# A planner's prices set anew: POOL's operations and waits, row sums on ScalarE, fp32r matmuls and array part changes

## The chip, the cores and the metric

One core of a Trainium2 chip runs the whole program. The metric is device time in microseconds (us), as the median of several executions; one further execution was taken by the hardware profiler, and all rows below are of that one. The engines are PE (TensorE; its weight loads are PEld), DVE (VectorE), ACT (ScalarE), POOL (GpSimd) and SP, which starts transfers. Each engine works through a queue of its own, strictly in order, and waits at an instruction whose inputs are not ready. So the order in which the program lists instructions decides who waits.

## The reference, cut to what matters

256 tokens of width 1024 go through two blocks.

```python
x = first_block(...)    # hybrid_mixer (SSD scan, attention, convolution), then 32 experts, top 2
return second_block(x, ...)   # rwkv7_time_mix, then diff_attention_mix
def rwkv7_time_mix(...):      # 16 heads of 64
    r, k, v, g = einsum(xmix, w_in);  kk = kk / maximum(norm(kk), 1e-12)
    state, y = scan(step, ...)
    y = (y - mean) * rsqrt(var + GN_EPS) * lnx_g + lnx_b     # per head
def diff_attention_mix(...):  # 8 heads of 2 x 64
    attn = softmax(s0) - lam * softmax(s1)
    o = rms_norm(attn @ v, subln_g) * (1 - lam_init)
h = h + rms_norm(y);  h = h + rms_norm(sigmoid(h @ ple_gate) * (p @ ple_w))
```

What matters here is that the second block has many small reciprocal roots: the norm of `kk` and the group norm in each pair of RWKV heads, and a norm in each attention head. No engine computes them in one instruction here; they are Newton steps.

## The kernel before, in words

Three parts follow each other. **The mixer** (`mixer`, L509) and **the second block** (`second`, L1577) are not written in the order in which they run. They are written as many generators ("streams"), each yielding instructions of one strand of work, and a planner picks the order. **The experts** (`moe`, L1189) between them are written in their order by hand.

The planner is the class `Plan` (L141) with the chooser `Mux` (L329). `Plan` keeps a time for every engine (`at`) and, for each tile region, when its last use ends. An instruction is ready (`ready`, L194, through `when`) at the latest end of what it depends on plus a handover from the table `LAT` (L145), which has one number for each pair of producing and consuming engine. It starts at the later of that and the engine's own time (`start`, L198); on TensorE the price of a change of array part (`change`, L261) comes on top. Its length is from `cost` (L213), in ns, and the table is worked out by engine:

```python
        if eng == "scalar":
            return (51 if psum else 93) + n * 0.835 + 93 * s.pointers(op)
        return 150 + n * 2.1                                    # POOL; n elements a partition
```

`Mux.run` (L362) looks at the head of every stream, finds the earliest planned start, and among the instructions of that engine that could start within a hold (60 ns for TensorE, 120 for DVE and ACT, 150 for POOL, `WAIT`, L54) takes the one of the highest rank. So a planned time is never waited for on the chip; it only decides the place in the queue. `come` (L204) leaves the price of a part change out once TensorE has been on the same kind (fp32 or fp32r) for longer than `LONG` (400 ns for fp32). A matmul's form is its rows and columns rounded to 32, 64 or 128 (`form`, L251).

Most operations are recorded at L76, the line where `Op.go` calls the engine, so tiles tell them apart.

In the second block, `Feed` (L1590) loads a raw weight slab, copies it on ACT to fp32r (`whl<-raw`) and subtracts on DVE for the low part (`whl<-raw,whl`). `dense` multiplies the slabs on TensorE into banks `pd`, at a low rank. The strands with high rank are the heads:

- `rwkv_inner` (eight pairs of heads): norms of `kk` into `nn` (matmuls against `tab`, form 128x64), a Newton step on POOL, then a spread of its result over partitions by matmuls `pm<-ident,rsq_y` (form 128x64).
- `rwkv_invert` and `rwkv_chunks`: a triangular inverse in 64x64 and 32x32 matmuls (`pi`), the chunked scan (`pe`), statistics `bn` on DVE, eight small operations and a Newton step on POOL for n below 6 (on DVE for 6 and 7), then `yn` on DVE and transposes `pe<-ident,yn`.
- `diff_head` (eight heads): scores into `pe`, `e` masked on DVE, exponentials with row sums on ACT, `on` squared with a row sum into `ss`, a Newton step (POOL for n below 6, else DVE), then `on` scaled on DVE and transposed on TensorE (`pi<-ident,on`).
- `Finish` (twice): projection, norms and gates; the product by the gain (`work<-e,gain`, 128x512) runs on POOL.

`newton` (L1670) on POOL is one start operation and three rounds of four, each depending on the one before: 13 small operations on tiles of 2 or 4 columns.

`minus` and `add` (L1643, L1655) could choose DVE or POOL by planned time, but return DVE when `s.alone` is true, as it is in both planned parts. They carry their own copy of POOL's price, which stays.

Of the kernel before, what the change touches and what calls it, by code (L numbers as in the profile page):

```python
# [140 lines left out]
class Plan:  # L141
# [1 line left out]


    LAT = {("vector", "vector"): 127, ("gpsimd", "gpsimd"): 100, ("scalar", "vector"): 133, ("vector", "scalar"): 128,  # L145
           ("scalar", "scalar"): 143, ("scalar", "gpsimd"): 159, ("vector", "gpsimd"): 155, ("gpsimd", "scalar"): 75,
           ("gpsimd", "vector"): 75, ("gpsimd", "tensor"): 200, ("scalar", "tensor"): 225, ("vector", "tensor"): 215,
           ("tensor", "scalar"): 197, ("tensor", "vector"): 197, ("tensor", "tensor"): 0}

# [63 lines left out]
    def cost(s, op):  # L213
        eng, name, out, ins = op.lane.name, op.op, op.outs[0], op.ins
        n = 1
        for _, c in (ins[-1] if name in ("tensor_reduce", "bn_stats") else out).ap[1:]:
            n *= c
        if eng == "tensor":
            if name == "transpose":
                return 109  # L220
            if ins[0].dtype == F32R:
                return max(107, n / 2.4) + 11
            k, m = s.form(op)
            if k == m:
                if k == 128:
                    return max(214, n * 4 / 2.4 + 4)
                return 58 if m == 64 else 31
            if k == 64:
                return max(107, n * 4 / 2.4) * (0.75 if n > 128 else 1) + 2
            if m == 64:  # L230
                return 58 if n < 8 else 165 if n <= 64 else 109
            return 13 if s.box(out)[0] else max(107, n * 2 / 2.4) + 14
        psum = any(x.space == PSUM for x in (out, *ins))
        if eng == "vector":
            fast = name in ("tensor_scalar", "tensor_copy", "memset") and not psum
            return 68 + n * (0.52 if fast else 1.04) + 61 * s.pointers(op)
        if eng == "scalar":
            return (51 if psum else 93) + n * 0.835 + 93 * s.pointers(op)
        if eng == "sync":
            return n * 512 / 355.0  # L240
        return 150 + n * 2.1

    @staticmethod
    def pointers(op):
# [16 lines left out]
    def change(s, op):  # L261

        op = getattr(op, "ops", [op])[0]
        if s.part is None or s.part == s.form(op) or (s.part, s.form(op)) == ((64, 128), (128, 128)):
            return 0
        return 138 if s.cold(s.at.get("tensor", 0.0)) else 95

    def clocked(s, start, dur, op):

# [2485 lines left out]
```

## Time and profile before

| what | us |
|---|---|
| median of 3 executions | 1253.44 |
| lowest, highest | 1244.65, 1255.34 |
| the profiled execution | 1252.17 |
| its span, first to last instruction | 1250.4 |
| busy in the span: PE / DVE / ACT / POOL | 1136.9 / 656.9 / 434.5 / 124.3 |

The span is the profiled execution without what lies around the program, 1.8 us. "Busy" is time in which an engine has an instruction in work; an engine's wait is put down to what ended it. The granted clock is TensorE's, as a share of 2.4 GHz: it has two levels, 1.00 and 0.50.

### The profile page before, as it was taken

The numbers are of one execution on the slowest core, as the hardware profiler recorded it, in microseconds if no ns is written. First come the engines' busy times: TensorE is split into PE (matmuls) and PEld (weight loads), VectorE is DVE, ScalarE is ACT, GpSimd is POOL, SyncE is SP. The second block draws the span as 40 slices with busy tenths as digits, with TensorE's granted clock in tenths as the row PEclk, the third lists the DMA queues.
The fourth block names the chain that finished last, engine by engine and source line by source line (L and its number), as shares of the span: only waits on it lengthen the run. The fifth ranks groups of instructions, "written<-read, shape, count | busy, mean of one in ns | idle before, by whom it ended". The sixth has DMA issues, their size and how long they took to land. (4 is left out here: it accounts for less than half of the span.)

```text
span 1250.4 us, 20460 instructions
## 1 busy us (share of the span) xinstructions
PE 1136.9 (91%) x7902; PEld 783.9 (63%) x7902; DVE 656.9 (53%) x1790; ACT 434.5 (35%) x1081; POOL 124.3 (10%) x358
## 2 busy tenths in 40 slices
PE   5999996999999999898987889999999978998896
PEld 3787786443443434443434788888887655888775
DVE  4586676121111111111113986677777658788785
ACT  3474452111111101110104564343436437455453
POOL 1000000000000000000000031222212011122202
PEclk9899998899999999999997798999999989999998
DMA  8668657799999999999994341122214422443332
GB/s 369 264 235 320 244 210 323 305 420 420 421 420 420 420 420 421 421 420 420 421 419 162 129 162 61 39 76 70 73 52 155 175 76 85 169 148 123 121 109 74
DMA packets 52628, 306.14 MB, mean 245 GB/s; under 512 B 5680, under 2 KB 10288, under 8 KB 25392
## 3 DMA queue, kind: packets, MB, share of 16 engines
q1 hardware_dynamic: 52368, 304.67, 61.7%
q8 instruction: 64, 1.05, 0.3%
q14 instruction: 36, 0.29, 0.1%
q0 software_dynamic: 160, 0.13, 0.1%
HBM read 302.55 MB, written 2.10 MB: 244 GB/s over the span
## 5 line engine op out<-in xcount | busy, mean ns | idle before, releaser
L411 PE MATMUL pgu<-w,xe 128*64 128x512 f32 x1024 | 232.3, 595 | 14.6 <-DMA w<-moe 14.6
L411 PEld LDWEIGHTS pgu<-w,xe 128*64 128x64 f32 x1024 | 80.0, 137 | 154.9 <-issue 116.8
L76 DVE TENSOR_TENSOR whl<-raw,whl 128x512 fp32r<-128x512 f32 x192 | 127.4, 688 | 7.7 <-ACT whl L76 6.5
L76 PE MATMUL pd<-xm,whl 128*128 128x256 f32 x768 | 122.5, 307 | 8.0 <-ACT xm L76 6.5
L76 ACT CAST whl<-raw 128x512 fp32r<-128x512 f32 x192 | 110.6, 619 | 49.0 <-PE pd L76 33.4
L411 PE MATMUL py<-w,condp 128*64 128x512 f32 x480 | 108.4, 596 | 7.0 <-ACT condp L1461 7.0
L76 PEld LDWEIGHTS pd<-xm,whl 128*128 128x128 f32 x768 | 105.7, 205 | 13.6 <-ACT xm L76 7.1
L1486 DVE SCALAR_TENSOR_TENSOR yl<-py,ws,yh 128x512 fp32r<-128x512 f32 (+1 forms) x33 | 24.2, 735 | 121.9 <-ACT yh L1485 121.9
L411 PEld LDWEIGHTS py<-w,condp 128*64 128x64 f32 x480 | 35.8, 137 | 69.2 <-issue 55.0
L1395 POOL TENSOR_TENSOR order<-P,wt 128x256 f32<-128x256 f32 x16 | 9.8, 615 | 615.3 <-PE pw L1466 419.5
L1485 ACT ACTIVATE yh<-py,ws 128x512 fp32r<-128x512 f32 (+1 forms) x33 | 22.1, 674 | 119.1 <-PE acc L411 65.5
L1451 DVE TENSOR_TENSOR condp<-condp,pgu 128x512 f32<-128x512 f32 x15 | 10.3, 687 | 97.6 <-PE pgu L411 97.6
L1450 DVE SCALAR_TENSOR_TENSOR condp<-condp,pgu 128x512 f32<-128x512 f32 x15 | 10.3, 688 | 95.3 <-ACT condp L1449 95.3
L76 PE MATMUL pd<-xx,whl 128*128 128x256 f32 x384 | 58.2, 290 | 1.9 <-ACT whl L76 1.1
L76 PE MATMUL pd<-hh,whl 128*128 128x256 f32 x384 | 58.4, 298 | 1.6 <-ACT whl L76 0.8
L76 PEld LDWEIGHTS pd<-hh,whl 128*128 128x128 f32 x384 | 51.3, 199 | 4.8 <-issue 2.4
L76 PE MATMUL pd<-whl,hh 128*128 128x512 f32 x192 | 52.1, 410 | 2.3 <-ACT hh L76 2.3
L76 PEld LDWEIGHTS pd<-xx,whl 128*128 128x128 f32 x384 | 50.3, 193 | 3.9 <-ACT whl L76 1.3
L76 PE MATMUL a<-hh,wh 128*128 128x256 f32 x160 | 47.7, 298 | 4.9 <-ACT wh L76 4.3
L76 DVE TENSOR_TENSOR wl<-w,wh 128x512 fp32r<-128x512 f32 (+1 forms) x60 | 39.1, 689 | 18.5 <-ACT wh L76 18.4
L76 PE MATMUL a<-hh,wl 128*128 128x256 f32 x160 | 47.4, 296 | 0.0
L76 PE MATMUL a<-hl,wh 128*128 128x256 f32 x160 | 46.8, 293 | 0.0
(511 smaller groups left out, 2187.0 us busy)
## 6 DMA issues: line engine op xcount, KB each, us to landing
w<-moe SPq DMA_DIRECT2D x190, 1024.0 KB, 19.8
w<-ada SPq DMA_DIRECT2D x12, 2048.0 KB, 11.6
raw<-awin SPq DMA_DIRECT2D x32, 512.0 KB, 3.3
raw<-bwin SPq DMA_DIRECT2D x32, 512.0 KB, 3.2
w<-win SPq DMA_DIRECT2D x5, 2048.0 KB, 9.3
raw<-pleg SPq DMA_DIRECT2D x16, 512.0 KB, 3.3
w<-wout SPq DMA_DIRECT2D x2, 2048.0 KB, 7.9
raw<-awout SPq DMA_DIRECT2D x8, 512.0 KB, 3.2
```

Of the source, the lines that this page charges most:

```text
L76: r = s.fn(*s.a, **s.k)
L411: return s.nc.tensor.matmul(out, lhsT=lhsT, rhs=rhs, start=first, stop=last, **kw)
L1395: G.tensor_tensor(PW.rearrange(four, e=2), P[:, :, o:o + 128].bitcast(F32).rearrange(four, e=2), wt[:, :, 2 * i:2 * i + 2, None].to_broadc ...
L1450: V.scalar_tensor_tensor(hid, hid, 1.0, pgu[0], op0=OP.add, op1=OP.mult)
L1451: V.tensor_tensor(hid, hid, pgu[1], op=OP.mult)
L1485: A.activation(y[0], p, AF.Copy, scale=ws)
L1486: V.scalar_tensor_tensor(y[1], p, ws, y[0].bitcast(F32), op0=OP.mult, op1=OP.subtract)
```

## The change

Five prices change: what POOL reads from ACT or DVE counts as ready 500 ns after its end; a POOL operation counts 170 ns plus its elements; an ACT operation with a second output (a row sum, `accum_out`) counts 92 ns more; an fp32r matmul counts its columns at 2.35 in place of 2.4 a ns; and at the upper clock a change of array part costs 115 ns out of 64x64, 60 out of 128x64 and 95 out of the others, in place of 95 for all.

```diff
     LAT = {("vector", "vector"): 127, ("gpsimd", "gpsimd"): 100, ("scalar", "vector"): 133, ("vector", "scalar"): 128,
-           ("scalar", "scalar"): 143, ("scalar", "gpsimd"): 159, ("vector", "gpsimd"): 155, ("gpsimd", "scalar"): 75,
+           ("scalar", "scalar"): 143, ("scalar", "gpsimd"): 500, ("vector", "gpsimd"): 500, ("gpsimd", "scalar"): 75,
...
             if ins[0].dtype == F32R:
-                return max(107, n / 2.4) + 11
+                return max(107, n / 2.35) + 11
...
         if eng == "scalar":
-            return (51 if psum else 93) + n * 0.835 + 93 * s.pointers(op)
+            return (51 if psum else 93) + n * 0.835 + 93 * s.pointers(op) + 92 * (len(op.outs) > 1)
         if eng == "sync":
             return n * 512 / 355.0
-        return 150 + n * 2.1
+        return 170 + n * 2.1
...
         if s.part is None or s.part == s.form(op) or (s.part, s.form(op)) == ((64, 128), (128, 128)):
             return 0
-        return 138 if s.cold(s.at.get("tensor", 0.0)) else 95
+        if s.cold(s.at.get("tensor", 0.0)):
+            return 138
+        return {(64, 64): 115, (128, 64): 60}.get(s.part, 95)
```

## Rows read from the trace of the kernel before

**Rows 1.** Busy time by stage: stretch, its length, busy us by engine, PEclk, DMA share, GB/s.
```profile
core 0: us, PE busy (x) PEld busy (x) DVE busy (x) ACT busy (x) POOL busy (x), PEclk, DMA share, GB/s
0.00:225.00 225.00, 194.79 (x1378) 159.62 (x1379) 146.71 (x472) 102.68 (x253) 6.41 (x17) 0.93 0.71 283
...
690.00:960.00 270.00, 257.36 (x2772) 220.91 (x2773) 209.40 (x585) 123.00 (x317) 63.20 (x233) 0.93 0.25 84
960.00:1085.00 125.00, 111.62 (x648) 83.46 (x648) 87.06 (x252) 63.23 (x156) 8.29 (x5) 0.95 0.38 133
1085.00:1200.00 115.00, 101.79 (x747) 90.54 (x745) 94.26 (x232) 59.96 (x182) 28.18 (x79) 0.97 0.37 127
1200.00:1250.40 50.40, 40.35 (x186) 31.89 (x185) 33.59 (x88) 20.72 (x47) 8.34 (x5) 0.94 0.27 94
```

**Rows 2.** Waits, PE from 1085 to 1200, DVE from 690: total, times, longest.
```profile
PE pi L76 <- DVE on L76: 11.0, 7, 2.1
...
DVE on L76 <- POOL rsq_y L76: 10.1, 6, 2.0
```

**Rows 3.** Waits of PE from 690 to 960.
```profile
PE pm L76 <- POOL rsq_y L76: 2.7, 1, 2.7
PE pe L76 <- DVE yn L76: 1.8, 3, 0.8
```

**Rows 4.** Timeline of one attention head: start, us, engine, operation, idle before.
```profile
1087.39 0.16 DVE L76 TENSOR_SCALAR ss<-ss 128x2 f32<-128x2 f32 x1
...
1090.61 0.68 DVE L76 TENSOR_TENSOR whl<-raw,whl 128x512 fp32r<-128x512 f32 x1
...
1087.63 0.55 POOL L76 TENSOR_SCALAR rsq_i<-ss 128x2 int32<-128x2 int32 x1 [42.25 <-DVE ss L76]
...
1090.62 0.72 POOL L76 TENSOR_TENSOR rsq_t<-rsq_t,ss 128x2 f32<-128x2 f32 x1
1091.43 0.19 POOL L76 TENSOR_SCALAR rsq_t<-rsq_t 128x2 f32<-128x2 f32 x1
...
1092.80 0.19 POOL L76 TENSOR_TENSOR rsq_y<-rsq_y,rsq_t 128x2 f32<-128x2 f32 x1
...
1093.60 0.41 PE L76 MATMUL pi<-ident,on 128*128 128x128 f32 x2 [2.06 <-DVE on L76]
1093.77 2.75 PE L76 MATMUL pd<-hh,whl 128*128 128x256 f32 x12
```

**Rows 5.** Timeline of POOL, first and last of an RWKV chunk's 21 operations.
```profile
852.88 0.20 POOL L76 TENSOR_TENSOR mu<-bn 128x4 f32<-128x4 f32 x1 [6.82 <-DVE bn L76]
...
858.74 0.20 POOL L76 TENSOR_TENSOR rsq_y<-rsq_y,rsq_t 128x4 f32<-128x4 f32 x1
```

**Rows 6.** Busy time and PEclk behind the wait, and PE's timeline later in that stage.
```profile
1093.95:1097.35 3.40, 3.40 (x17) 2.78 (x15) 2.02 (x4) 1.77 (x6) 0.00 (x0) 0.50 0.28 83
...
1162.32 2.13 PE L76 MATMUL pd<-hh,whl 128*128 128x256 f32 x9
...
1129.12 3.14 PE L76 MATMUL pd<-hh,whl 128*128 128x256 f32 x24
```

**Rows 7.** The chain that ended last: start, us, what.
```profile
743.50 4.47 PE pd L76 x27
...
1233.70 6.91 PE pd L76 x30
```

**Rows 8.** Groups of POOL and ACT: count, busy us, mean ns, idle before.
```profile
L76 POOL TENSOR_TENSOR work<-e,gain 128x512 f32<-128x512 f32 x8 | 10.7, 1340 | 31.1 <-DVE e L76 31.1
...
L76 ACT ACTIVATION_READ_ACCUMULATOR e<-e,mx 128x1 f32 x32 | 6.0, 187 | 0.0
```

**Rows 9.** Timeline of PE: one spread of eight whole, another in three pieces.
```profile
749.61 0.66 PE L76 MATMUL pm<-ident,rsq_y 128*64 128x128 f32 x8
...
845.89 0.43 PE L76 MATMUL pm<-ident,rsq_y 128*64 128x128 f32 x2
...
847.66 0.43 PE L76 MATMUL pm<-ident,rsq_y 128*64 128x128 f32 x2
...
848.93 0.44 PE L76 MATMUL pm<-ident,rsq_y 128*64 128x128 f32 x4
```

## Prediction

> **What bounds the kernel now.** I read the busy times by stage first [rows 1]. The program has three parts: the mixer (to 225 us), the experts (225 to 690) and the second block (690 to the end). TensorE (PE) is busy 195 of 225 us in the first and 511 of 560 in the last, so it is the bound there and only its idle time, or a slower clock, can be won. The experts' order is written by hand and reads none of the numbers that change. The mixer uses POOL for 6.4 us in all. In the second block POOL works 63 us in the RWKV stage (690 to 960) and 28 us in the heads of the differential attention (1085 to 1200). What the new numbers can move is there.
>
> Next I read who waits for whom. In the heads PE stands 11.0 us in seven waits for `on`, and DVE stands 10.1 us in six waits for POOL's `rsq_y`, right ahead of `on` [rows 2]. In the RWKV stage PE waits once 2.7 us for `rsq_y`, and three times, 1.8 us in all, for `yn`, which reads a `rsq_y` too [rows 3]. With six sevenths of the 11.0 (one of those heads has its Newton step on DVE) 2.7 + 1.8 + 9.4 = 13.9 us of PE stand behind POOL.
>
> The timeline of one head shows why [rows 4]. DVE ends `ss` at 1087.55 (1087.39 + 0.16), and POOL's thirteen operations of the Newton step end at 1092.99: 5.44 us. The planner of before counts 155 + 13 x 154 + 12 x 100 = 3.36 us (a 128x2 operation is 150 + 2 x 2.1 ns). So it lists `on` 2.1 us too early in DVE's queue and `ident,on` as early in PE's. Both engines work their queues in order, so DVE stands (one of the six waits above), and PE stands 2.06 us with work listed behind that could have run, twelve projections `pd`.
>
> **The change part by part.** No instruction is added or removed, and none changes its engine: the two helpers that choose between DVE and POOL always return DVE, since `s.alone` is true in both planned parts. Only the order on each engine moves.
>
> *POOL's wait and POOL's operations.* What POOL reads from DVE or ACT counts as ready 500 ns after its end instead of 155 or 159, and each POOL operation counts 20 ns more. A head's Newton step is planned 345 + 13 x 20 = 605 ns later, at 3.97 of the 5.44 us that it takes. For an RWKV chunk, eight small operations and a Newton step, the plan was 155 + 9 x 158 + 12 x 258 = 4.67 us and becomes 500 + 9 x 178 + 12 x 278 = 5.44; the trace has 852.88 to 858.94, 6.06 us [rows 5]. So both plans stay short, but less. The 500 ns are not the trace's handover (1087.55 to 1087.63, under 0.1 us), they stand in for slow first operations of 0.55 us; the pace of a step is right: from 1091.43 to 1092.80 five steps take 0.274 us each [rows 4], the new number is 174 + 100.
>
> In the heads, then, six waits get shorter by at most 0.605, 3.6 us. PE has work to put in, since the `pd` behind `ident,on` wait for nothing that is late. What speaks against the whole 3.6 is in the same rows: a POOL operation takes 0.72 us while DVE runs `whl<-raw,whl`, the first one 0.55, and 0.19 once DVE stands still [rows 4]. If DVE fills its gap with one more `whl`, one POOL operation becomes 0.36 to 0.53 us longer; at 0.4, six chains give 2.4 us back. The filler may also read PSUM, or be none, so I take half of that: 3.6 - 1.2 = 2.4 us, ends 0 and 3.6.
> The Trainium skill (SBUF — State Buffer, section "Who interferes with whom") says that a DVE instruction with two inputs in SBUF contends with a POOL instruction that reads SBUF, and that of the two sharing a port pair the second waits out the first. This trace agrees, with 0.72 us beside `whl` and 0.19 alone. By that rule a constant price for POOL cannot be right in both states, and a slot that is filled lengthens what it was to wait out: with every slot so filled the heads would win 1.2 us, without it 3.6.
>
> *The clock behind the longest waits.* After the wait of 2.06 us the granted clock of the next 3.4 us is 0.50, its lower level of 1.2 GHz: twelve `pd` take 2.75 us, and behind the fifth wait nine take 2.13, where 24 take 3.14 at the upper level, 0.13 each [rows 4, 6]. That is 2.75 - 1.57 = 1.2 and 2.13 - 1.18 = 0.95 us. Shorter waits may spare these 2.1 us; half is 1.0, ends 0 and 2.1.
>
> *RWKV.* The wait of 2.7 us shrinks by 0.6. The 27 `pd` in the chain behind it take 4.47 us, 0.166 each [rows 7], for 0.13: 1.0 us of clock, which I count at half, for a wait of 2.1 would be as long as those after which the clock fell. Of the three `yn` waits (1.8 us) I take 1.2; the plan moves by 0.77 each, which covers them unless others come. Together 0.6 + 0.5 + 1.2 = 2.3 us, ends 0 and 4.
>
> *The products by gain on POOL in the two finishing stages.* Eight, planned at 1.23 us plus 0.155, now 1.25 plus 0.5, measured 1.34 [rows 8] after a handover under 0.1: planned 0.3 us too late rather than too early. Their reader waits for a sum of squares and a Newton step of DVE besides, which hides it. Cost zero; with the cover gone, 8 x 0.3 = 2.4 us lost.
>
> *Row sums on ScalarE.* 92 ns more for each activation with a sum. The trace has the reading of the sum as an operation of its own, 187 ns [rows 8], partly beside the activation, so 92 is nearer than nothing. It shifts the heads' exponentials by 0.18 us a pair. Zero, ends -1 and +1 us.
>
> *Fp32r matmuls* (N / 2.35 in place of N / 2.4). 256 columns go from 118 to 120 ns, 512 from 224 to 229; thirty 512-column ones take 6.91 us, 230 each [rows 7]. PE's planned time gets right by 2%; by itself that moves nothing. The mixer is touched by this and the sums alone, and PE stands 30 us there [rows 1], mostly for weights and chains with nothing to fill in. Zero, ends -3 and +3 us, a tenth of that.
>
> *Changes of array part.* 115 ns out of 64x64 and 60 out of 128x64, each 95 before. The price only decides which of several ready matmuls goes first. Zero; what it can cost is rival C.
>
> Sum: 2.4 + 1.0 + 2.3 = 5.7 us. Not all of it gets to the end: the finishing stages (960 to 1085, and from 1200) are chains in which PE stands 13.4 and 10.1 us, and DVE is busy 82% in the heads [rows 1]. I count nine tenths, 5.1 us. The profiled execution has 1252.17 us, 1.8 more than its span of 1250.4, and the median shown is 1.3 above it. So 1247.1 for such an execution, and by the median **1248 us**.
>
> **Rivals.**
> *A. Given back.* The waits for POOL keep their length because DVE's filler blocks POOL, or the next stage waits by as much. For it: slow POOL operations stand beside DVE work [rows 4]. Against: some 0.4 is given back for 0.605. Gain 0 to 1 us: 1253. The skill's rule above is this rival.
> *B. The waits go.* A shift lets all 13.9 us behind POOL go, with 3.1 us of the lower clock: 1253 - 17 = 1236. For it: filler lies right behind each wait. Against: the new plan is still 1.5 us short in each head.
> *C. Slower, by broken batches.* PE's window for preferring a higher stream is 60 ns. A price of 95 kept a 128x64 batch whole against it; 60 does no longer. Place: the RWKV heads' `st` and spread batches and the chunks' pairs, some ten seams in each of eight heads, 80. Price: a spread of eight takes 0.66 us whole; broken into 2, 2 and 4 it takes 0.43 + 0.43 + 0.44 = 1.30 [rows 9], so 0.32 a break. From 16 further breaks on the forecast's gain is gone; 30 give 1248 + 9.6 = 1258, all 80 give 1274. Against: batches are broken already, and the planner drops the price after 400 ns on the same kind of matmul.
> That the change does nothing would need every order to stay; 605 ns are five `pd`, so it won't.
>
> **How the numbers follow.** Forecast (a gain of 1 to 12 us) 0.46, A 0.20, B 0.16, C 0.18. One per cent, 12.5 us, is about what a measurement of this kernel can tell from no change. Faster by that: 0.14 of B and 0.08 of the forecast's and the mixer's far ends, 0.22. Slower by that: half of C, 0.09. Same: 0.69. The range goes from just under B, 1235, to 1261, which holds C up to 40 breaks and the unknown costs of the mixer and of the gain products.
>
> **What would show it.** Right: PE's waits for `on` near 8 us instead of 11.0, DVE's for `rsq_y` near 7 instead of 10.1, more `pd` ahead of `ident,on`, no fall of the clock behind the heads' waits. By A POOL's slow operations become more and the waits stay. By C the 128x64 groups stand in more and shorter pieces from 690 to 960, and that stage is longer. I am wrong if the difference sits in the mixer, or if the RWKV stage moves by over 5 us either way.

## The result, and the profile after

The changed kernel takes 1235.9 us (median of 4, 1233.2 to 1238.8) where the kernel before takes 1251.8 beside it: ratio 0.9883, 95% interval 0.9857 to 0.9909. That is 15 us less, 11 to 18 by the interval, where the prediction had 5. The profiled execution has a span of 1237.1 us, 13.3 less than before.

No instruction was added or removed, so the first thing to compare is what the same instructions cost. The page's busy times of the changed kernel:

```profile
PE 1125.5 (91%) x7902; PEld 774.2 (63%) x7902; DVE 656.2 (53%) x1790; ACT 434.4 (35%) x1081; POOL 121.9 (10%) x358
```

TensorE's 7902 matmuls take 11.4 us less (1136.9 before); its idle time, span less busy, went from 113.5 to 111.6. So of 13.3 us about 11.4 are the same matmuls running quicker and only 1.9 are waits. Added up from the clock records, TensorE spent 112.1 us of the whole span at its lower level before and 88.6 after. The prediction had looked for waits first.

To see where, I cut both traces at the same events: the first operation of the experts, the first projection `pd`, the end of the last `yn`, and, as bounds of the attention heads, the first matmul `xx,whl` and the first matmul `whl,hh` behind the last `on`. Busy times in the three stretches that count (mixer; RWKV; heads): the stretch, its length, PE, PEld, DVE, ACT, POOL, granted clock, DMA. The kernel before:

```profile
0.00:219.95 219.95, 190.58 (x1358) 155.38 (x1358) 145.60 (x470) 101.84 (x251) 5.79 (x16) 0.94 0.71 281
690.53:1002.18 311.65, 297.49 (x3042) 247.47 (x3043) 237.70 (x683) 140.58 (x354) 63.20 (x233) 0.94 0.28 97
1051.31:1206.13 154.82, 136.98 (x991) 122.11 (x992) 124.24 (x312) 84.09 (x246) 28.18 (x79) 0.97 0.39 135
```

The changed kernel:

```profile
0.00:217.97 217.97, 187.95 (x1358) 153.39 (x1358) 145.14 (x470) 101.73 (x251) 5.81 (x16) 0.97 0.72 284
688.82:993.13 304.31, 289.66 (x3043) 240.19 (x3043) 236.93 (x682) 140.78 (x355) 60.40 (x233) 0.96 0.30 99
1040.62:1192.48 151.86, 136.19 (x991) 122.28 (x992) 124.67 (x312) 84.34 (x246) 29.24 (x79) 0.97 0.42 137
```

The mixer is 2.0 us shorter, RWKV 7.3, the heads 3.0; the pieces between and behind give the rest. In the mixer TensorE's idle time (length less PE busy) did not fall either, 29.4 before and 30.0 after. In RWKV it is 14.2 before and 14.7 after: nothing was won on waits there. Its busy time fell by 7.8 us for one and the same 3042 or 3043 matmuls, and the granted clock rose from 0.94 to 0.96. In the heads it is the other way round: the clock is 0.97 in both, and idle went from 17.8 to 15.7.

The waits that answer to [rows 2] and [rows 3], of the changed kernel, waits in total, times, longest:

```profile
PE pi L76 <- DVE on L76: 8.6, 6, 1.8
...
DVE on L76 <- POOL rsq_y L76: 8.2, 6, 1.6
...
PE pm L76 <- POOL rsq_y L76: 2.0, 1, 2.0
```

And the head of [rows 4] after the change:

```profile
1077.18 0.17 DVE L76 TENSOR_SCALAR ss<-ss 128x2 f32<-128x2 f32 x1
...
1077.44 0.56 POOL L76 TENSOR_SCALAR rsq_i<-ss 128x2 int32<-128x2 int32 x1 [43.35 <-DVE ss L76]
...
1082.43 0.19 POOL L76 TENSOR_TENSOR rsq_y<-rsq_y,rsq_t 128x2 f32<-128x2 f32 x1
...
1082.66 0.42 DVE L76 TENSOR_TENSOR on<-pq,rsq_y 128x256 f32<-128x256 f32 x1 [0.82 <-POOL rsq_y L76]
...
1083.23 0.41 PE L76 MATMUL pi<-ident,on 128*128 128x128 f32 x2 [0.83 <-DVE on L76]
```

Here DVE waits 0.82 us and PE 0.83, where PE waited 2.06. POOL's thirteen operations take about as long as they did (5.18 us from the first start to the last end, 5.36 before); other work now stands ahead of `on`.

### The profile page after: what moved, and what is told of

Same layout as the page of the kernel before. It is cut to its first block, busy times and chain, and to the rows that moved or that the text cites. A ratio compares the mean times of both kernels' runs of the same rounds, so it can differ in the third digit from the quotient of the medians.

```text
span 1237.1 us, 20470 instructions
## 1 busy us (share of the span) xinstructions
PE 1125.5 (91%) x7902; PEld 774.2 (63%) x7902; DVE 656.2 (53%) x1790; ACT 434.4 (35%) x1081; POOL 121.9 (10%) x358
## 5 line engine op out<-in xcount | busy, mean ns | idle before, releaser
L413 PE MATMUL pgu<-w,xe 128*64 128x512 f32 x1024 | 232.3, 595 | 14.7 <-DMA w<-moe 14.7
L76 PE MATMUL pd<-xm,whl 128*128 128x256 f32 x768 | 117.7, 301 | 8.1 <-ACT xm L76 6.6
L76 PEld LDWEIGHTS pd<-xm,whl 128*128 128x128 f32 x768 | 102.5, 200 | 13.4 <-ACT xm L76 7.2
L1453 DVE TENSOR_TENSOR condp<-condp,pgu 128x512 f32<-128x512 f32 x15 | 10.3, 688 | 97.7 <-PE pgu L413 97.7
L1452 DVE SCALAR_TENSOR_TENSOR condp<-condp,pgu 128x512 f32<-128x512 f32 x15 | 10.3, 689 | 95.4 <-ACT condp L1451 95.4
## 6 DMA issues: line engine op xcount, KB each, us to landing
w<-wout SPq DMA_DIRECT2D x2, 2048.0 KB, 10.5
```

Source lines behind the costliest of these rows:

```text
L76: r = s.fn(*s.a, **s.k)
L413: return s.nc.tensor.matmul(out, lhsT=lhsT, rhs=rhs, start=first, stop=last, **kw)
L1452: V.scalar_tensor_tensor(hid, hid, 1.0, pgu[0], op0=OP.add, op1=OP.mult)
L1453: V.tensor_tensor(hid, hid, pgu[1], op=OP.mult)
```

## The experiments

I held three theories. P: the waits behind POOL are what was won, so POOL's prices alone do it. J: the prices together make the plan right, and any order planned from them is good. R, later narrowed to S: some of it belongs to single prices, and the rest is what this one order happens to draw.

### Each price alone

```diff
e1: -("scalar", "gpsimd"): 159, ("vector", "gpsimd"): 155    +500, 500;   -return 150 + n * 2.1   +return 170 + n * 2.1
e2: -return 138 if s.cold(...) else 95                       +{(64, 64): 115, (128, 64): 60}.get(s.part, 95) when not cold
e3: -max(107, n / 2.4) + 11                                  +max(107, n / 2.35) + 11
e4: -(51 if psum else 93) + n * 0.835 + ...                  +... + 92 * (len(op.outs) > 1)
```

> The kernel before with POOL's two prices alone changed (500 ns of wait, 170 ns an operation). Theory P (the waits behind POOL are what was won): it takes most of the 14.6 us, ratio near 0.990; DVE's waits for rsq_y in the heads near 8 us as in the changed kernel, and the RWKV stage shorter by 5 to 7 us. Theory R (any new order of this kernel moves the time by several us either way, and the sum of the parts is not the whole): heads about 2.5 us shorter, RWKV stage anywhere within 5 us of before, ratio 0.993 to 1.002.

> The kernel before with the prices of array part changes alone changed (115 out of 64x64, 60 out of 128x64). Theory P: no part of the gain, within 2 us of before. The third rival of the prediction: slower by up to 10 us, with the 128x64 groups in more pieces. Theory R: within 6 us of before either way, all of it in the RWKV stage; the waits behind POOL unchanged.

> The kernel before with the price of fp32r matmuls alone changed (2.35 for 2.4). Theory P: within 2 us of before. Theory M (the mixer's 1.7 us and some of the RWKV stage come from TensorE's planned time, that is now right by 2%): the mixer 1.5 to 2 us shorter and in all 3 to 6 us faster. Theory R: within 6 us either way.

> The kernel before with the price of ScalarE's row sums alone changed (92 ns more). Theory P: within 2 us of before, the heads at most 0.5 us shorter, RWKV unchanged, since only the heads, the finishing stages and the mixer have such sums. Theory R: the same bound of 2 us in the heads, but the mixer may move by 2 us.

Measured against the kernel before: POOL's prices 0.9994 (0.9972 to 1.0015), part changes 0.9995 (0.9971 to 1.0019), fp32r 1.0049 (1.0028 to 1.0071), sums 1.0003 (0.9983 to 1.0023). Three are nothing and one is slower, and together they are 0.9883. P falls, and so does any account in which the parts add up. So does M, the theory held for e3 that the fp32r price wins 3 to 6 us by itself. With POOL's prices alone DVE's waits for `rsq_y` did fall to 8.1 us and the heads to 146.9 us, 8 less; but RWKV came out at 318.3, 7 more, beyond the 5 that R had allowed. With the sums alone the mixer came out at 226.5, 7 more where R had allowed 2. With the part price alone the heads came out at 148.7, 6 less, though R had put all of a change into RWKV; the waits behind POOL are as before there (10.2), and TensorE was 3 us at its lower level in place of 10.

Rival C of the prediction falls as well: in the RWKV stretch the 128x64 matmuls stand in 54 unbroken runs before, in 59 with the part price alone and in 53 in the changed kernel. Few batches were broken, and the time did not move.

### The same kernel again, and one nanosecond

```diff
e5: (no difference to the changed kernel)
e6: -("vector", "vector"): 127     +("vector", "vector"): 128
```

> The changed kernel itself once more. If the stretches at TensorE's lower clock belong to the order of the work, they come back at the same places (15 us of them in the mixer, 23 in the RWKV stage, against 27 and 35 before) and the ratio is again near 0.988; if they belong to the execution, they fall elsewhere and the stage lengths move by some us.

> The changed kernel with the handover from DVE to DVE at 128 ns in place of 127, a difference without any meaning that still makes another order. Theory R (the gain is what this one order happens to draw): it moves by 3 to 10 us, most likely upwards, ratio 0.991 to 1.000. Theory J (the prices together make the plan right, and any order from them is good): ratio 0.986 to 0.991, within 3 us of the changed kernel.

The changed kernel again: 0.9875 (0.9848 to 0.9902), so the gain is real and repeats. With one nanosecond more on a handover of 127: 1242.1 us, 0.9919 (0.9894 to 0.9944), 6 to 7 us slower than the changed kernel. The RWKV stretch of e5, and then that of e6:

```profile
687.07:989.12 302.05, 286.84 (x3043) 237.39 (x3043) 237.79 (x682) 140.82 (x355) 60.11 (x233) 0.97 0.31 100
```

```profile
689.25:999.94 310.69, 294.38 (x3043) 243.02 (x3043) 238.78 (x682) 141.22 (x355) 61.86 (x233) 0.96 0.30 97
```

The price of e6 is no better and no worse than the one of the changed kernel, and its RWKV stage is where before's was (311.6). Theory J, which asked for a time within 3 us of the changed kernel, falls for this stage; R had 3 to 10 us, most likely upwards.

### One price taken back

```diff
e7: -("scalar", "gpsimd"): 500, ("vector", "gpsimd"): 500    +159, 155;   -170 + n * 2.1   +150 + n * 2.1
e8: -max(107, n / 2.35) + 11                                 +max(107, n / 2.4) + 11
```

> The changed kernel with POOL's two prices as before. Theory P or J: 5 to 8 us slower than the changed kernel (the waits for rsq_y back at 10 us in the heads, and those of RWKV), ratio 0.993 to 0.995. Theory R: heads 2 to 3 us longer and the rest anywhere, ratio 0.987 to 1.000.

> The changed kernel with the fp32r price as before. Alone that price made the kernel 0.5% slower. If parts add up, taking it out gives 6 us more, ratio near 0.983. Theory J: it loses the mixer's 1.7 us and more, ratio 0.990 to 0.994. Theory R: anywhere from 0.985 to 1.000.

Without POOL's prices 1.0065 (1.0041 to 1.0088), beyond what I had allowed: waits for `rsq_y` back at 10.6 us, heads 157.2, and RWKV at 314.5 with 20.4 us of idle PE. Of the 157.2 some 5 are no loss: cut at the same events, this stretch holds 1014 matmuls where the others have 981 to 994, and ten matmuls of the kind that moved into it take 2.44 us in the kernel before. Without the fp32r price 0.9981 (0.9959 to 1.0002): the mixer is at 221.1, and RWKV at 313.4. The fp32r price that costs 0.5% alone is worth 1% in this company; e11, below, loses as much by 0.01 in the same price, so this can be a draw of the order too.

### Two prices, a longer wait for POOL, and two more neighbours

```diff
e9:  the kernel before with e1's and e3's edits
e10: the changed kernel,  -("scalar", "gpsimd"): 500, ("vector", "gpsimd"): 500    +1800, 1800
e11: the changed kernel,  -n / 2.35    +n / 2.36
e12: the kernel before,   -("vector", "vector"): 127    +128
```

> The kernel before with the fp32r price and POOL's two prices changed, sums and part changes as before. Theory S (the fp32r price wins some 4 us in the mixer, POOL's prices some 4 us in the heads, and the RWKV stage is a draw): mixer 216 to 219 us, heads 147 to 152 where before has 155, waits for rsq_y near 8.2; the RWKV stage between 302 and 318, so ratio 0.988 to 1.001. Theory J (all four belong together): RWKV 302 to 305 only with all four, so here 0.995 or above.

> The changed kernel with 1800 ns in place of 500 for what POOL reads from DVE or ACT, so that a head's Newton step is planned at 5.3 us, as long as the trace shows it. Theory S: DVE's waits for rsq_y in the heads fall from 8.2 to below 2.5 us and PE's for on from 8.6 to below 3, heads 145 to 149; mixer as in the changed kernel; the RWKV stage a draw between 302 and 318. If a filled gap blocks POOL instead, the waits stay above 5 us.

> The changed kernel with 2.36 in place of 2.35 for fp32r matmuls, half a nanosecond in 110 that still makes another order from 700 us on and nearly the same one in the mixer. Theory S: mixer within 1 us of the changed kernel's 216 to 218, heads 147 to 152, RWKV a draw between 302 and 318, most likely longer. Theory J: everything within 3 us of the changed kernel.

> The kernel before with the handover from DVE to DVE at 128 ns in place of 127. Theory S: the mixer 219 to 224 us, with 20 us or more at the lower clock; waits for rsq_y in the heads still 10 to 11 us, heads 152 to 158; the RWKV stage between 302 and 318; ratio 0.993 to 1.007. If the mixer falls to 217 here too, its gain was a draw as well.

Measured: e9 1.0103 (1.007 to 1.0136), e10 0.9896 (0.9861 to 0.993), e11 0.9978 (0.9959 to 0.9996), e12 1.0008 (0.9986 to 1.0029). e9 is slower than S's forecast (J had 0.995 or above), RWKV 322.8 and the mixer 223.2. e11 and e12 came as S had them in every stage; J had e11 within 3 us of the changed kernel, and it is 1247.5 us. e10 shows the mechanism that the prediction described. Its waits in the heads:

```profile
PE pi L76 <- DVE on L76: 2.2, 4, 0.8
...
DVE on L76 <- POOL rsq_y L76: 2.6, 2, 1.4
```

With a price at which a Newton step is planned as long as it is, the waits behind it all but end (11.0 and 10.1 before), and the heads take 142.3 us for 154.8, with 8.9 us of idle PE for 17.8. S had the waits below 3 and 2.5 us and the heads at 145 to 149. (Some 1.4 us of the gain are five or six matmuls which this order puts behind the stretch.) Its RWKV stage, then its heads:

```profile
686.78:998.63 311.85, 296.08 (x3043) 244.71 (x3043) 235.54 (x682) 139.79 (x355) 66.71 (x233) 0.95 0.29 97
1047.01:1189.36 142.35, 133.50 (x986) 120.35 (x986) 122.40 (x309) 81.05 (x241) 30.15 (x79) 0.98 0.42 142
```

Of the 9.5 us won in the heads against the changed kernel 7.5 are lost again in RWKV and most of the rest behind these stretches, and the whole is the same. No run beat the changed kernel.

### What the fourteen profiles say together

Lengths of the three stretches, cut in the same way, and in brackets the time that TensorE spent there at its lower level, added up from the clock records of each trace, all in us:

| kernel | mixer | RWKV | heads | DVE's waits for `rsq_y` in the heads |
|---|---|---|---|---|
| before | 219.9 (27) | 311.6 (35) | 154.8 (10) | 10.1 |
| e12, before, 1 ns | 221.1 (22) | 307.8 (26) | 154.3 (14) | 10.3 |
| e2, part alone | 221.6 (26) | 313.2 (29) | 148.7 (3) | 10.2 |
| e3, fp32r alone | 216.5 (20) | 315.3 (28) | 157.8 (17) | 10.7 |
| e4, sums alone | 226.5 (36) | 309.8 (33) | 153.7 (14) | 10.0 |
| e7, no POOL price | 217.4 (15) | 314.5 (35) | 157.2 (10) | 10.6 |
| e1, POOL alone | 221.7 (29) | 318.3 (47) | 146.9 (3) | 8.1 |
| e8, no fp32r price | 221.1 (27) | 313.4 (28) | 149.9 (10) | 6.2 |
| e9, fp32r and POOL | 223.2 (31) | 322.8 (48) | 154.4 (17) | 8.5 |
| changed | 218.0 (15) | 304.3 (23) | 151.9 (10) | 8.2 |
| e5, changed again | 216.4 (16) | 302.1 (16) | 151.3 (10) | 8.3 |
| e6, changed, 1 ns | 218.5 (15) | 310.7 (26) | 146.9 (7) | 8.2 |
| e11, changed, 2.36 | 215.9 (15) | 310.3 (23) | 148.7 (3) | 9.7 |
| e10, changed, 1800 ns | 216.1 (15) | 311.9 (33) | 142.3 (7) | 2.6 |

*Heads.* The seven profiles with POOL's prices (e10, which goes further, left out) have 150.0 us in the mean, the six without have 154.4. Not all of these 4 us are the prices' own: single profiles overlap (e2 without them has 148.7, e9 with them 154.4), the time at the lower level goes from 3 to 17 us, and e7 holds more work. Idle PE is the nearer measure: 15.0 us in the mean with the prices, 16.8 without, 17.8 to 15.7 from before to changed, 8.9 in e10. So some 2 us are shown to be the prices' own.

*Mixer.* The six profiles with both the fp32r price and the sums have 217.1 us in the mean and 15 or 16 at the lower level; the eight that lack one or both have 221.5. POOL's prices and the part price change nothing in the mixer: its instructions stand in the same order on every engine in before, e1 and e2, in e3 and e9, and in e4 and e8 (no run has the fp32r price and the sums alone). The six are one order as well, but for e11's matmuls. One order still spreads by execution, 216.5 and 223.2 us in e3 and e9, 226.5 and 221.1 in e4 and e8. The trace shows the two places. In the kernel before, ACT has a cast of a weight tile listed ahead of the copy of `adasb`; the cast waits for its DMA, the copy stands behind it, and TensorE's spread of `adasb` waits for the copy. ACT's timeline, then TensorE's:

```profile
53.32 0.62 ACT L76 CAST wh<-w 128x512 fp32r<-128x512 f32 x1 [1.53 <-DMA w<-win]
53.85 0.58 ACT L76 COPY adasb<-x 128x512 f32<-128x512 f32 x1
```

```profile
54.48 1.05 PE L76 MATMUL x<-sel,adasb 128*128 128x1 f32 x8 [1.35 <-ACT adasb L76]
...
56.21 0.34 PE L76 MATMUL a<-wh,hl 128*128 128x268 f32 x1
56.35 0.43 PE L76 MATMUL a<-wh,hh 128*128 128x268 f32 x1
```

From 56.3 us, 1.8 behind the end of that wait, each matmul of 268 columns starts 0.22 us after the last in place of 0.12: the clock is at its lower level for 3.4 us. In the changed kernel the copy follows activations that are ready, ahead of the next cast, and the spread does not wait:

```profile
50.16 0.59 ACT L76 COPY adasb<-x 128x512 f32<-128x512 f32 x1 [0.65 <-PE x L76]
50.64 1.59 ACT L76 ACTIVATE hh<-xc,mod,ga 128x256 fp32r<-128x256 f32 x3
```

```profile
50.90 0.95 PE L76 MATMUL x<-sel,adasb 128*128 128x1 f32 x8
```

All eight profiles of kernels with the fp32r price lack this wait for the copy, and all six without it have it, 1.35 to 1.68 us; in all six the clock falls behind it, in none of the eight does it fall there. Near 170 us the fp32r price without the sums leaves one wait of 2.62 us (e3 and e9) and a fall behind it; with the sums it is split (the longest is 1.28 in the changed kernel) and the clock stays. So the two prices do belong together there. What was won is not the waits themselves: idle PE in the mixer is 29.4 us before and 30.0 after, busy time 190.6 and 188.0, the time at the lower level 27 and 15.

*RWKV.* 302 to 304 in two profiles of the one changed order, 308 to 323 in the twelve others, whatever their prices. One of the twelve, e4, has before's order of matmuls in this stage, and 309.8 us. From before to changed the clock is most of it. Twelve `pd` take 2.75 us at the lower level for 1.57 at the upper [rows 4, 6], so 1 us there is worth 0.43: of the 7.3 us some 5 are 12 us less at the lower level, idle PE is 0.5 more, and the rest of TensorE's busy time is some 2.6 less. The clock falls in this stage behind a wait, as behind POOL's first one in all fourteen, or in runs of small matmuls between the projections (at 790.2 and 916.5 us in the kernel before, with no idle time just ahead). The places are not the order's alone: e5 is the changed kernel itself and has 16 us at the lower level there against 23, and e3 and e9 have the same order of matmuls in the mixer and 20 against 31. Which feature of the changed order spares it falls stays open.

The clock does not explain the neighbours. In the table the last column counts where a matmul takes another part of the array (its rows and columns, rounded as `form` does) than the one before it:

| kernel | RWKV | idle PE | at the lower level | changes of array part |
|---|---|---|---|---|
| before | 311.6 | 14.2 | 35 | 299 |
| e4, before's order | 309.8 | 13.7 | 33 | 299 |
| e12, before, 1 ns | 307.8 | 13.9 | 26 | 299 |
| changed | 304.3 | 14.7 | 23 | 292 |
| e5, changed again | 302.1 | 15.2 | 16 | 292 |
| e6, changed, 1 ns | 310.7 | 16.3 | 26 | 301 |
| e11, changed, 2.36 | 310.3 | 15.7 | 23 | 318 |

The stretch of e11:

```profile
686.58:996.90 310.32, 294.58 (x3042) 242.10 (x3043) 238.18 (x683) 140.52 (x354) 64.06 (x233) 0.96 0.28 97
```

It has the changed kernel's time at the lower level and is 6.0 us longer, 1.0 of it idle and 4.9 in busy time. Nor is it the one execution: all ten of e11 have a granted clock of 0.964 to 0.968, like the four of the changed kernel, and take 1247.5 us for 1235.9. The order changes the array part 26 times more. In the kernel before, a matmul behind one of 64x64 starts 148 ns after it when the part changes and some 50 when it does not, behind a 128x128 one of 256 columns 209 and 120 (medians at the upper level). At 0.1 us that makes 2.6 of the 4.9 us, by estimate; the rest stays open. So the changed order is good in two ways, in its falls of the clock and in what its matmuls take at the upper level, and a neighbour can lose either: e6 loses 1.6 in idle time, some 1.5 by the clock and 3.3 in the rest.

## Why the prediction was right or wrong

The direction, the range (1235 to 1261) and the mechanism in the heads hold; the size does not: 5 us forecast, 15 measured, and I called "faster by over 1%", which came by the ratio (0.9883, though its interval reaches 0.9909), 0.22. That the range holds 1235.9 is luck: its lower end was set just under rival B, and B is not what happened.

*The heads.* Forecast: 2.4 us less waiting, PE's waits near 8 us and DVE's near 7. Measured: PE's 11.0 to 8.6, DVE's 10.1 to 8.2, idle PE 17.8 to 15.7, the stretch 3.0 us shorter. The term was right. (One of the seven waits, the 0.5 us of the head whose Newton step is on DVE, went altogether; the six sevenths that I had counted as POOL's, 9.4, were 10.5.) What DVE's filler gives back was counted at 0.2 us a chain; POOL's steps last 5.34 us in the mean of six after the change and 5.19 before, 0.15. Rival A is at work, but small: 33 of 78 operations last over 0.4 us, 29 before.

*The clock behind the longest waits.* Forecast 1.0 us; measured none: 10 us at the lower level in the heads before and after, with a fall behind two of the waits for `on` in both. The fall behind POOL's first wait of the RWKV stage, which I counted at half, is there in all fourteen profiles.

*RWKV.* Forecast 2.3 us, from the waits for `rsq_y` and `yn`. The one wait fell from 2.7 to 2.0 as forecast, and the three waits for `yn` (1.8) went, but another of 1.9 us came at 992.8, and idle PE in the stage did not fall (14.2 and 14.7). Measured: 7 to 9 us, most of it from the clock and some 2 from the matmuls' other busy time. This is the step that failed. I had the clock as a consequence of POOL's waits only; in this stage TensorE has 35 us at the lower level before, worth some 15, and a new order redraws it, as it redraws the changes of array part, a term that I had put at zero. The prediction's own test says so: "I am wrong if the difference sits in the mixer, or if the RWKV stage moves by over 5 us either way."

*The mixer.* Forecast zero, ends -3 and +3. Measured 2 us, and 4 over the means: a change of 2% in TensorE's planned time was enough to bring ACT's copy of `adasb` out from behind a cast that waits for its DMA. The wait of 1.35 us went, but idle PE in all did not fall (29.4 and 30.0); PE's busy time fell by 2.6, and of the 12 us less at the lower level 6.8 are the falls behind that wait and near 170 us. "By itself that moves nothing" was wrong.

*Three rivals.* B's time of 1236 came, but not by B: 8.6 and 2.0 us of the waits behind POOL are still there. A holds only for RWKV's waits. C is excluded by e2 and by the count of runs, and its price of 0.32 us a break was too high: it adds up the lengths of pieces that overlap their neighbours, where from start to start a matmul behind a 128x64 one comes at 152 ns when the part changes and 58 when it does not.

So of the 15 us some 2 to 3 in the heads and 2 to 4 in the mixer come with the changed prices in the neighbours too (e6 and e11); the 7 to 9 of RWKV are the draw of one order, which one nanosecond in a price gives back. Whether the prices make good orders more likely there is not shown by so few neighbours.

## What to carry to other kernels

Where a planner orders the work, compare the changed kernel with neighbours that differ by a meaningless nanosecond before crediting the change: here both neighbours of the changed kernel lost 6 us in one stage. Split a gain into idle time and busy time of the same instructions; if busy time fell, it is not the waits, and the time at the lower clock and the count of part changes tell how much each of them can explain. A price that is set to the trace does what it should at its own place (the heads, with the wait priced in full: DVE's waits 10.1 to 2.6 us), so judge it by the waits there and not by the total.

## What was not expected of the hardware

The granted clock fell to its lower level at different places in two executions of one order: in RWKV 23 us in one profile and 16 in the next, in the mixer 20 and 31 for one order of matmuls. Nor does the length of a wait alone tell whether a fall follows. Behind the heads' waits for `on` the clock fell after 2.06 and 2.04 us and stayed after 1.77 and 1.73 in the kernel before; in the changed one it fell after 1.75 and 1.73 and stayed after 1.58 and 1.55; in the mixer 1.35 us were followed by 3.4 us at the lower level. e12 has before's order of matmuls in the heads, and there the clock stayed after the same waits of 2.07 and 2.03 and fell after 1.73 and 1.89.
